# q and k projections of the seven-product blocks, computed token-major and transposed on TensorE

## The chip, the cores and the metric

The kernel runs on one core of a Trainium2 chip. The metric is the device time of one execution in microseconds (us). Three runs of the kernel before took 979.81, 979.97 and 980.25 us, with a median of 979.97.

## What is computed

One encoder layer on 512 tokens of width 2048, in f32. One input projection of 8192 columns gives q, k, v and a gate for each of two groups of 16 heads (head size 64):

```python
h = jnp.einsum('bsd,de->bse', x, w_in[layer])
qa, ka, va, ga, qb, kb, vb, gb = jnp.split(h, splits, axis=-1)
ya = _dilated_attention(heads(qa, N_HEADS_A), heads(ka, N_HEADS_A), heads(va, N_HEADS_A), t5_bias)
yb = _neighbourhood_attention(heads(qb, N_HEADS_B), heads(kb, N_HEADS_B), heads(vb, N_HEADS_B), na_rpb[layer])
ya = merge(ya) * jax.nn.silu(ga.astype(jnp.float32))
yb = merge(yb) * jax.nn.silu(gb.astype(jnp.float32))
y = jnp.concatenate([ya, yb], axis=-1).astype(x.dtype)
out = jnp.einsum('bse,ed->bsd', y, w_out[layer])
x = _layer_norm(DEEPNORM_ALPHA * x + out, ln_gain[layer], ln_bias[layer])
```

Group A attends over strided windows, group B over a two-dimensional neighbourhood. This case concerns only the projections to q and k of both groups: four matrices of 2048 x 1024, each multiplied with the 512 tokens.

## The kernel before

**Precision.** Each f32 operand of a large product is split into a high part (a rounded copy, made on ACT) and a low part (the rest, made on DVE), and a product is three matmuls: high x high, high x low, low x high. The function `split` and the helpers `high` (L364) and `low` (L369) do this.

**Stages.** Up to 71.03 us x is loaded and split and the first six gate tiles are computed (`plain_block`). Then come six seven-product blocks up to 546.82 us, in the order k, q, v of group A and k, q, v of group B. Behind them stand the attention, filled up with the other gate tiles (L516) and the first part of the output projection (L710), and last the rest of the output projection and the norm.

**A seven-product block** (`strassen_block`) cuts the matrix, the tokens and the depth into halves and needs seven products of half size instead of eight. The sums of halves of x are made once (`combine`); the sums of weights are made on DVE (L360) as each product comes up. A product has 8 depth slices of 128, handled in four steps of two (`run`, u = 0 to 3), and fills two PSUM banks, `accs[0]` and `accs[1]`. A block so has 28 steps.

In a v block the stationary operand is a slice of x (128 tokens) and 512 weight columns move: 12 matmuls a step (L384 to L386), and a bank holds 128 tokens x 512 channels. In a k or q block the stationary operand is a slice of the weights (128 channels) and 256 tokens move: 24 matmuls a step (L391 to L393), and a bank holds two tiles of 128 channels x 256 tokens. For k the tokens move in another order, (r b c) instead of (b r c), through a stepped read of x.

**The results.** The seven products are summed into four quarters of the result, named r1, w, u3 and c22, each in one SBUF tile with two halves t (`pair`). `keep` copies the first product on ACT, `combine_` makes four subtractions a half on DVE behind the fourth product (L406), and `plus` adds the fifth, sixth and seventh (L440). `store_kq` then splits a half into high and low (ACT and DVE) and writes it to DRAM, channel-major, with four transfers on SP's queue. The attention reads q and k from there.

**The order of the work** on PE, DVE and ACT is written out by hand (`manual_schedule` around `run_blocks`). At step n the loop issues the addition of weights for step n+3, ACT's high part for step n+2, then what `at` has put down for this step (the list `behind`), DVE's low part for step n+2, and last the matmuls of step n. There are three pairs of high and low buffers (`halves`), so ACT's copy for step n+2 waits for the matmuls of step n-1. SP and POOL are ordered by the planner of the language. PSUM has four buffers in `pacc`, two in `pss` and two in `pst` (the name pt); of the products, only the fourth in time (number 6) lies in `pst`, until `combine_` has read it.

Of the kernel before, what the change touches and what calls it, by code (L numbers as in the profile page):

```python
# [25 lines left out]
HALF = 256  # L26
# [44 lines left out]
def hybrid_layer(tc, xT, xn, w_in, w_early, w_gate, w_out, t5x, brow, rpb, cmask, eye, gain, lbias, out):  # L71
    nc = tc.nc
    from contextlib import ExitStack
    with ExitStack() as ctx:
# [6 lines left out]
        pst = ctx.enter_context(tc.tile_pool(name="pst", bufs=2, space=bass.MemoryType.PSUM))  # L81
# [44 lines left out]
        ident = const.tile([128, 128], F32, name="ident")  # L126
# [118 lines left out]
                        to = q_d[g][4 * ch + 2 * b + n][i].rearrange("c (b h q) -> c h b q", b=4, h=2)[:, half]  # L245
                        nc.sync.dma_start(to, f(o[:, i, n].rearrange("p (b q) -> p b q", b=4)))

        def store(kind, g, ch, half, t, src):
            if kind == "v":
                store_v(g, ch, half, t, src)  # L250
            else:
                store_kq(kind, g, ch, half, t, src)

        def silu(o, acc):

# [83 lines left out]
        jobs, behind = [], {}  # L339

        def strassen_block(src, kind, g, hooks):

            base = len(jobs)

            def load(q, tags):
                def run():
                    for u in range(4):
                        raw = slot(tags[u], F32, "braw")
                        nc.sync.dma_start(raw, src[4 * q + u])
                        raws[q].append(raw)  # L350
                return run

            raws = {q: [] for q in range(4)}

            def product(i, pool, q, other=None):
                accs = []

                def add(u):
                    if other is not None:
                        nc.vector.tensor_tensor(raws[q][u], raws[q][u], raws[other][u], ALU.add)  # L360

                def high(u):
                    h = halves.next("wh", F32R)
                    nc.scalar.activation(h, raws[q][u], AF.Copy)  # L364
                    return h

                def low(u, h):
                    l = halves.next("wl", F32R)
                    nc.vector.tensor_tensor(l, raws[q][u], f(h), ALU.subtract)  # L369
                    return h, l  # L370

                def run(u, h, l):
                    if u == 0:
                        accs.extend(bank(pool, "acc") for _ in range(2))
                    for t in range(2):
                        for kk in range(2):
                            k = 2 * u + kk
                            ah, al = operand(i, k)
                            if kind == "k":
                                ah, al = (m.rearrange("p (b r c) -> p r b c", r=4, b=4) for m in (ah, al))  # L380
                            if kind == "v":
                                c = slice(512 * kk, 512 * kk + 512)
                                q = slice(128 * t, 128 * t + 128)
                                nc.tensor.matmul(accs[t], ah[:, q], h[:, c], start=k == 0, stop=False)  # L384
                                nc.tensor.matmul(accs[t], al[:, q], h[:, c], start=False, stop=False)  # L385
                                nc.tensor.matmul(accs[t], ah[:, q], l[:, c], start=False, stop=k == 7)  # L386
                                continue
                            for n in range(2):
                                c = slice(512 * kk + 256 * t + 128 * n, 512 * kk + 256 * t + 128 * n + 128)
                                o = accs[t][:, HALF * n:HALF * n + HALF]  # L390
                                nc.tensor.matmul(o, h[:, c], ah, start=k == 0 and n == 0, stop=False)  # L391
                                nc.tensor.matmul(o, h[:, c], al, start=False, stop=False)  # L392
                                nc.tensor.matmul(o, l[:, c], ah, start=False, stop=k == 7 and n == 1)  # L393
                    if u == 3:
                        next(hooks, lambda: None)()

                jobs.extend((lambda u=u: add(u), lambda u=u: high(u), lambda h, u=u: low(u, h),
                             lambda h, l, u=u: run(u, h, l)) for u in range(4))
                return accs

            def at(product_, u, fn):

                behind.setdefault(base + 4 * product_ + u, []).append(fn)

            def sub(o, x, y):
                nc.vector.tensor_tensor(o, x, y, ALU.subtract)  # L406
# [24 lines left out]
            def combine_(t):  # L431
                r1, w, u3, c22 = (pair(n)[t] for n in ("r1", "w", "u3", "c22"))
                sub(w, r1, p6[t])
                sub(u3, w, p7[t])
                sub(c22, p5[t], u3)
                sub(w, p5[t], w)

            def plus(name, p, t):
                o = pair(name)[t]
                nc.vector.tensor_tensor(o, p[t], o, ALU.add)  # L440

            for t in range(2):
                at(1, t, lambda t=t: keep(t))
                at(4, t, lambda t=t: combine_(t))
                for n, name, p in ((5, "w", p3), (6, "r1", p2), (7, "u3", p4)):
                    at(n, t, lambda t=t, name=name, p=p: plus(name, p, t))
            for t in range(2):
                for n, name, ch, half in ((4, "c22", 1, 1), (5, "w", 1, 0), (6, "r1", 0, 0), (7, "u3", 0, 1)):
                    at(n, t + 1, lambda t=t, name=name, ch=ch, half=half: store(kind, g, ch, half, t, pair(name)[t]))
            sets[0], sets[2] = sets[2], sets[0]  # L450

        def run_blocks():
            ready = []
            for n in range(-4, len(jobs) + 4):
# [576 lines left out]
```

## Time and profile before

| | |
|---|---|
| median of 3 runs | 979.97 us |
| span of the profiled execution, first to last instruction | 978.4 us |
| PE busy | 968.1 us (99%) |
| DVE busy | 756.8 us (77%) |
| ACT busy | 486.6 us (50%) |
| six seven-product blocks | 71.03 to 546.82 us |
| mean granted TensorE clock | 0.996 |

The profile gives the profiled execution by its span of 978.4 us; the median of the runs lies 1.6 us above it. Busy time of PE counts a matmul from its start to a modelled end, and matmuls overlap: what a matmul costs in a full stream is the distance from its start to the next one's. Rows of the timeline show the start, the length, the engine, the line, the operation, the names out<-in, the shape and the count of merged instructions. Rows of the windows show the stretch, its length, busy time and count by engine (PE, weight loads PEld, DVE, ACT, POOL), the clock, the share of the DMA engines and GB/s.

### The profile page before, as it was taken

Reading aid. Unit: us, or ns where it says so; the run is one execution under the profiler, and the core shown is the slowest. Engines: PE = TensorE matmul, PEld = TensorE weight load, DVE = VectorE, ACT = ScalarE, POOL = GpSimd, SP = SyncE. Lnnn points to the kernel's source line nnn. Section 1 sums busy time; section 2 is a strip of 40 time slices with the busy share of each in tenths; the row PEclk is TensorE's granted clock in tenths of the full one; section 3 lists DMA queues with packets and bytes.
Section 4 is the critical chain, followed back from the end, with each engine's and each line's share of the span. In section 5 each row is a group of like instructions: output and inputs, shape, how many; then the busy total and the mean of one; then the engine's idle time right before and its main releaser. Section 6 shows DMA issues by size and latency. Waiting matters only on the chain.

```text
span 978.4 us, 16019 instructions
## 1 busy us (share of the span) xinstructions
PE 968.1 (99%) x5851; PEld 855.0 (87%) x5851; DVE 756.8 (77%) x1152; ACT 486.6 (50%) x839; POOL 179.0 (18%) x327
## 2 busy tenths in 40 slices
PE   9999999999999999999999999999999999999996
PEld 6889999999888999999888888888888888888885
DVE  7947788788988977878889567676676767777877
ACT  7534344344444434434454366666666666762300
POOL 1000665664553400000000001010010000100021
PEclk9999999999999999999999999999999999999998
DMA  9731688599569638428634967777777788768322
GB/s 341 289 120 55 164 276 270 177 255 273 178 188 302 185 95 277 116 87 232 165 120 113 343 185 217 194 232 234 188 222 224 197 238 205 209 223 293 90 75 97
DMA packets 118014, 194.29 MB, mean 199 GB/s; under 512 B 48351, under 2 KB 67551, under 8 KB 117936
## 3 DMA queue, kind: packets, MB, share of 16 engines
q1 hardware_dynamic: 105104, 169.15, 56.6%
q0 software_dynamic: 12256, 23.47, 8.7%
q8 instruction: 46, 0.75, 0.3%
q10 hardware_dynamic: 576, 0.66, 0.2%
q14 instruction: 32, 0.26, 0.1%
HBM read 148.68 MB, written 44.50 MB: 197 GB/s over the span
## 4 chain that ended last, share of the span: by engine, by line
PE 96%; DVE 1%; ACT 1%; DMA 1%; issue 0%; SPq 0%; DVEq 0%; ACTq 0%
PE acc L710 15%; PE acc L516 11%; PE acc L391 11%; PE acc L393 11%; PE acc L392 11%; PE acc L384 5%; PE acc L386 5%; PE acc L385 5%; PE pv L662 4%; PE pt L640 4%; PE acc L270 2%; PE sc L621 2%; PE acc L272 2%; PE acc L271 2%; PE sc L620 2%; PE sc L710 1%
## 5 line engine op out<-in xcount | busy, mean ns | idle before, releaser
L364 ACT ACTIVATE wh<-braw 128x1024 fp32r<-128x1024 f32 x168 | 178.3, 1061 | 254.9 <-PE acc L392 130.9
L369 DVE TENSOR_TENSOR wl<-braw,wh 128x1024 fp32r<-128x1024 f32 x168 | 206.4, 1229 | 65.6 <-ACT wh L364 65.3
L391 PE MATMUL acc<-xk,wh 128*128 128x256 f32 x512 | 144.5, 282 | 0.0
L393 PE MATMUL acc<-xk,wl 128*128 128x256 f32 x512 | 144.4, 282 | 0.0
L392 PE MATMUL acc<-xk,wh 128*128 128x256 f32 x512 | 144.4, 282 | 0.0
L360 DVE TENSOR_TENSOR braw<-braw 128x1024 f32<-128x1024 f32 x96 | 118.8, 1237 | 0.0
L710 PE MATMUL acc<-wh,yk 128*128 128x512 f32 x320 | 108.4, 402 | 0.0
L392 PE MATMUL acc<-op,wh 128*128 128x256 f32 x384 | 108.4, 282 | 0.0
L391 PE MATMUL acc<-op,wh 128*128 128x256 f32 x384 | 108.3, 282 | 0.0
L393 PE MATMUL acc<-op,wl 128*128 128x256 f32 x384 | 108.3, 282 | 0.0
L646 DVE TENSOR_TENSOR tl<-pt,th 128x256 fp32r<-128x256 f32 (+1 forms) x128 | 71.1, 555 | 48.0 <-ACT th L645 46.8
L391 PEld LDWEIGHTS acc<-xk,wh 128*128 128x128 f32 x512 | 97.2, 190 | 0.9 <-ACT bias L150 0.9
L392 PEld LDWEIGHTS acc<-xk,wh 128*128 128x128 f32 x512 | 97.2, 190 | 0.1
L393 PEld LDWEIGHTS acc<-xk,wl 128*128 128x128 f32 x512 | 97.2, 190 | 0.0
L645 ACT ACTIVATE th<-pt 128x256 fp32r<-128x256 f32 (+1 forms) x128 | 62.3, 489 | 65.0 <-PE pt L640 62.9
L516 PE MATMUL acc<-xk,wh 128*128 128x512 f32 x320 | 90.8, 402 | 0.0
L577 DVE CUSTOM_DVE_ANT_0 s<-sc,biases 128x512 f32<-128x512 f32 (+2 forms) x128 | 68.1, 532 | 17.9 <-PE sc L621 17.3
L581 ACT ACTIVATE p<-s,mn 128x512 f32<-128x512 f32 (+1 forms) x96 | 62.1, 647 | 25.6 <-DVE mn L577 25.2
L392 PEld LDWEIGHTS acc<-op,wh 128*128 128x128 f32 x384 | 72.9, 190 | 0.0
L393 PEld LDWEIGHTS acc<-op,wl 128*128 128x128 f32 x384 | 72.9, 190 | 0.0
L391 PEld LDWEIGHTS acc<-op,wh 128*128 128x128 f32 x384 | 72.9, 190 | 0.0
L710 PEld LDWEIGHTS acc<-wh,yk 128*128 128x128 f32 x320 | 58.4, 189 | 9.1 <-ACT yk L694 0.3
(183 smaller groups left out, 2026.1 us busy)
## 6 DMA issues: line engine op xcount, KB each, us to landing
braw<-in_w_in SPq DMA_DIRECT2D x96, 512.0 KB
wraw<-in_w_out SPq DMA_DIRECT2D x32, 512.0 KB
wraw<-in_w_gate SPq DMA_DIRECT2D x20, 512.0 KB
k_d<-kst SPq DMA_DIRECT2D x64, 128.0 KB
q_d<-kst SPq DMA_DIRECT2D x64, 128.0 KB
v_d<-vst SPq DMA_DIRECT2D x32, 256.0 KB
q<-q_d SPq DMA_DIRECT2D x32, 256.0 KB
k<-k_d SPq DMA_DIRECT2D x16, 512.0 KB
```

The source lines that it names most:

```text
L360: nc.vector.tensor_tensor(raws[q][u], raws[q][u], raws[other][u], ALU.add)
L364: nc.scalar.activation(h, raws[q][u], AF.Copy)
L369: nc.vector.tensor_tensor(l, raws[q][u], f(h), ALU.subtract)
L391: nc.tensor.matmul(o, h[:, c], ah, start=k == 0 and n == 0, stop=False)
L392: nc.tensor.matmul(o, h[:, c], al, start=False, stop=False)
L393: nc.tensor.matmul(o, l[:, c], ah, start=False, stop=k == 7 and n == 1)
L516: nc.tensor.matmul(acc, w[:, k * 128:k * 128 + 128], X[8 * u + k][:, s], start=u == 0 and n == 0 and k == 0, stop=u == 1 and n == 2 and k ...
L577: nc.vector.tensor_tensor_reduce(*flat, bias, 1.0, 3e38, ALU.add, ALU.min, mn)
L581: nc.scalar.activation(p[:, to:to + n].rearrange("p (b r c) -> p b r c", r=8, c=c), s[:, :n].rearrange(order, r=8, c=c), AF.Exp, bias=mn, ...
L645: nc.scalar.activation(th, pt[:, :nch], AF.Copy)
L646: nc.vector.tensor_tensor(tl, pt[:, :nch], f(th), ALU.subtract)
L710: nc.tensor.matmul(acc[:, part], yk[k][:, s, c], w[:, wk], start=first and kk == 0 and n == 0, stop=last and kk == 1 and n == 2)
```

## The change

All six blocks now compute token-major, as v did: x is stationary, 512 weight columns move, 12 matmuls a step. The seven products are summed as before, now with 128 tokens on the partitions and 512 channels in a row. For q and k each finished quarter is turned to channel-major by PE: for each of two groups b of 256 channels, four transposes of 128x128 write one PSUM bank `pt` (`turned_out`). For k they write the tokens in the order (r b c), in runs of 16 elements. `store_kq` reads that bank instead of the SBUF tile. The transposes of group b stand three steps behind the first addition to the quarter's half b, the store four steps; for v the store stays one step behind.

```diff
+        def turned_out(kind, two, b):
+            pt = bank(pst, "pt")
+            for n in range(2):
+                o = pt[:, HALF * n:HALF * n + HALF]
+                c = slice(256 * b + 128 * n, 256 * b + 128 * n + 128)
+                for t in range(2):
+                    if kind == "k":
+                        to = o.rearrange("p (r b c) -> p b r c", r=4, b=4)[:, 2 * t:2 * t + 2]
+                    else:
+                        to = o[:, 128 * t:128 * t + 128]
+                    nc.tensor.transpose(to, two[t][:, c], ident)
+            return pt
...
-                            if kind == "k":
-                                ah, al = (m.rearrange("p (b r c) -> p r b c", r=4, b=4) for m in (ah, al))
-                            if kind == "v":
-                                c = slice(512 * kk, 512 * kk + 512)
-                                q = slice(128 * t, 128 * t + 128)
-                                nc.tensor.matmul(accs[t], ah[:, q], h[:, c], start=k == 0, stop=False)
-                                nc.tensor.matmul(accs[t], al[:, q], h[:, c], start=False, stop=False)
-                                nc.tensor.matmul(accs[t], ah[:, q], l[:, c], start=False, stop=k == 7)
-                                continue
-                            for n in range(2):
-                                c = slice(512 * kk + 256 * t + 128 * n, 512 * kk + 256 * t + 128 * n + 128)
-                                o = accs[t][:, HALF * n:HALF * n + HALF]
-                                nc.tensor.matmul(o, h[:, c], ah, start=k == 0 and n == 0, stop=False)
-                                nc.tensor.matmul(o, h[:, c], al, start=False, stop=False)
-                                nc.tensor.matmul(o, l[:, c], ah, start=False, stop=k == 7 and n == 1)
+                            c = slice(512 * kk, 512 * kk + 512)
+                            q = slice(128 * t, 128 * t + 128)
+                            nc.tensor.matmul(accs[t], ah[:, q], h[:, c], start=k == 0, stop=False)
+                            nc.tensor.matmul(accs[t], al[:, q], h[:, c], start=False, stop=False)
+                            nc.tensor.matmul(accs[t], ah[:, q], l[:, c], start=False, stop=k == 7)
...
+            outs = {}
+            def turn_out(name, b):
+                outs[name, b] = turned_out(kind, pair(name), b)
             for t in range(2):
                 for n, name, ch, half in ((4, "c22", 1, 1), (5, "w", 1, 0), (6, "r1", 0, 0), (7, "u3", 0, 1)):
-                    at(n, t + 1, lambda t=t, name=name, ch=ch, half=half: store(kind, g, ch, half, t, pair(name)[t]))
+                    if kind == "v":
+                        at(n, t + 1, lambda t=t, name=name, ch=ch, half=half: store_v(g, ch, half, t, pair(name)[t]))
+                        continue
+                    at(n, t + 3, lambda t=t, name=name: turn_out(name, t))
+                    at(n, t + 4, lambda t=t, name=name, ch=ch, half=half: store_kq(kind, g, ch, half, t, outs.pop((name, t))))
...
-            for n in range(-4, len(jobs) + 4):
+            for n in range(-4, len(jobs) + 8):
```

How the order of instructions changes is shown at three places of the first k block. The first is PE's queue where the fifth product ends and the sixth begins. Before:

```order
L391 MATMUL acc<-op,wh 128x256
L392 MATMUL acc<-op,wh 128x256
L393 MATMUL acc<-op,wl 128x256
L391 MATMUL acc<-xk_106,wh 128x256
L392 MATMUL acc<-xk_106,wh 128x256
```

Of the change, with xk_106 the slice of x that the sixth product begins with and c_1153 the quarter c22:

```order
L389 MATMUL acc<-wh,op 128x512
L390 MATMUL acc<-wh,op 128x512
L391 MATMUL acc<-wl,op 128x512
L259 MATMUL pt<-ident,c_1153 128x2x4x16 x4
L389 MATMUL acc<-wh,xk_106 128x512
L390 MATMUL acc<-wh,xk_106 128x512
```

A group of four transposes now stands between the matmuls of two steps; its sisters for the other channel group stand 12 matmuls earlier, and the next two groups (w) 36 and 48 matmuls later.

The second place is DVE's queue from the last subtractions of `combine_` on. Before:

```order
L406 TENSOR_TENSOR c_1345<-acc,u_1344 128x512
L406 TENSOR_TENSOR w<-acc,w 128x512
L88 TENSOR_TENSOR kst<-c_1345,kst 128x512
L369 TENSOR_TENSOR wl<-braw,wh 128x1024
L88 TENSOR_TENSOR kst<-c_1345,kst 128x512
L369 TENSOR_TENSOR wl<-braw,wh 128x1024 x2
L440 TENSOR_TENSOR w<-acc,w 128x512
L369 TENSOR_TENSOR wl<-braw,wh 128x1024
```

Of the change:

```order
L404 TENSOR_TENSOR c_1153<-acc,u_1152 128x512
L404 TENSOR_TENSOR w<-acc,w 128x512
L377 TENSOR_TENSOR wl<-braw,wh 128x1024 x3
L438 TENSOR_TENSOR w<-acc,w 128x512
L88 TENSOR_TENSOR kst<-pt,kst 128x512
L377 TENSOR_TENSOR wl<-braw,wh 128x1024
```

The split of the stored quarter (kst) has left the place between the subtractions and the weights' split (wl) and stands three steps later, behind an addition.

The third place is SP's queue, where the first k block stores and the next block's weights are loaded. Before:

```order
L349 DMA braw<-in_w_in 128x1024 x7
L243 DMA k_d<-kst 64x2x256 x8
L349 DMA braw<-in_w_in 128x1024 x2
L243 DMA k_d<-kst 64x2x256 x4
L349 DMA braw<-in_w_in 128x1024
```

Of the change:

```order
L357 DMA braw<-in_w_in 128x1024 x8
L243 DMA k_d<-kst 64x2x256 x4
L357 DMA braw<-in_w_in 128x1024
L243 DMA k_d<-kst 64x2x256 x4
L357 DMA braw<-in_w_in 128x1024 x5
```

The stores have moved behind weight loads that they stood ahead of. The rest of SP's queue keeps its order but for such shifts between stores and loads; POOL's queue is the same.

More of the change, by code (lines that the diff above doesn't have):

```diff
@@ L246, in store_kq @@
                         nc.sync.dma_start(to, f(o[:, i, n].rearrange("p (b q) -> p b q", b=4)))
-        def store(kind, g, ch, half, t, src):
-            if kind == "v":
-                store_v(g, ch, half, t, src)
-            else:
-                store_kq(kind, g, ch, half, t, src)
+        def turned_out(kind, two, b):
[10 more added lines that the diff above has]
+            return pt
         def silu(o, acc):
@@ L378, in run @@
                             ah, al = operand(i, k)
-                            if kind == "k":
-                                ah, al = (m.rearrange("p (b r c) -> p r b c", r=4, b=4) for m in (ah, al))
-                            if kind == "v":
-                                c = slice(512 * kk, 512 * kk + 512)
-                                q = slice(128 * t, 128 * t + 128)
-                                nc.tensor.matmul(accs[t], ah[:, q], h[:, c], start=k == 0, stop=False)
-                                nc.tensor.matmul(accs[t], al[:, q], h[:, c], start=False, stop=False)
-                                nc.tensor.matmul(accs[t], ah[:, q], l[:, c], start=False, stop=k == 7)
-                                continue
-                            for n in range(2):
-                                c = slice(512 * kk + 256 * t + 128 * n, 512 * kk + 256 * t + 128 * n + 128)
-                                o = accs[t][:, HALF * n:HALF * n + HALF]
-                                nc.tensor.matmul(o, h[:, c], ah, start=k == 0 and n == 0, stop=False)
-                                nc.tensor.matmul(o, h[:, c], al, start=False, stop=False)
-                                nc.tensor.matmul(o, l[:, c], ah, start=False, stop=k == 7 and n == 1)
+                            c = slice(512 * kk, 512 * kk + 512)
[3 more added lines that the diff above has]
+                            nc.tensor.matmul(accs[t], ah[:, q], l[:, c], start=False, stop=k == 7)
                     if u == 3:
```

## The prediction

> **What bounds the kernel now.** First the page: busy shares, then the chain of waits by engine.
>
> ```profile
> PE 968.1 (99%) x5851; PEld 855.0 (87%) x5851; DVE 756.8 (77%) x1152; ACT 486.6 (50%) x839; POOL 179.0 (18%) x327
> ...
> PE 96%; DVE 1%; ACT 1%; DMA 1%; issue 0%; SPq 0%; DVEq 0%; ACTq 0%
> ```
>
> PE is the chain: whatever PE is spared is time, whatever it is given is time, and work on other engines counts only once PE waits for it. So I cut the stage that changes into its six blocks, with the table of windows: from the first product matmul of a block to that of the next, in the order k, q, v, k, q, v.
>
> ```profile
> core 0: us, PE busy (x) PEld busy (x) DVE busy (x) ACT busy (x) POOL busy (x), PEclk, DMA share, GB/s
> 71.03:152.55 81.52, 81.52 (x678) 79.85 (x676) 65.51 (x67) 35.93 (x41) 33.50 (x69) 1.00 0.61 179
> 152.55:233.18 80.63, 80.63 (x675) 80.63 (x673) 65.40 (x67) 34.83 (x38) 48.83 (x98) 1.00 0.80 239
> 233.18:309.37 76.19, 76.19 (x339) 63.07 (x337) 66.57 (x67) 34.88 (x38) 38.90 (x63) 1.00 0.75 221
> 309.37:390.00 80.63, 80.63 (x673) 80.63 (x672) 66.70 (x67) 34.80 (x38) 12.84 (x23) 1.00 0.61 189
> 390.00:470.63 80.63, 80.63 (x674) 80.63 (x673) 65.33 (x67) 34.83 (x38) 0.00 (x0) 1.00 0.54 158
> 470.63:546.82 76.19, 76.19 (x338) 63.07 (x337) 67.59 (x75) 37.77 (x46) 1.90 (x2) 1.00 0.49 146
> ```
>
> Every block keeps PE busy throughout at full clock. A k or q block is 672 matmuls of 256 moving columns: 80.63/672 = 0.1200 us each. A v block is 336 of 512: 76.19/336 = 0.2268. The same multiplications thus cost 4.44 us less in v's form; solved for both widths, a matmul costs 0.0132 us beside 0.417 ns a column, and 336 of these fixed parts go.
>
> The first k block is odd: the bias matmuls of L149 stand inside it.
>
> ```profile
> 93.95 0.28 PE L393 MATMUL acc<-op,wl 128*128 128x256 f32 x1
> 94.16 1.89 PE L149 MATMUL sc<-bias 33*16 33x512 f32 x4
> 95.98 0.39 PE L391 MATMUL acc<-xk,wh 128*128 128x256 f32 x1
> 96.20 0.28 PE L392 MATMUL acc<-xk,wh 128*128 128x256 f32 x1
> ```
>
> From 93.95 to 96.20 are 2.25 us for two matmuls that take 0.24, so the insertion costs 2.01. Without it the block takes 79.51 us, 1.12 under its sisters: a small bonus that the new form has no row for, so I let it go.
>
> **The change part by part.** *Removed and added matmuls.* Four blocks take v's form. Before they hold 81.52 + 3 x 80.63 = 323.41 us; in the new form 4 x 76.19 + 2.01 = 306.77. Saved: 16.64 us. The v windows measure exactly this, so I give it +-0.5 (the bonus of 1.12 and the insertion are its soft parts).
>
> A page speaks against this term. The Trainium skill, "TensorE: Matmul & The Clock Gate", section "Back-to-back issue gap", gives a warm gap of N/2.4 ns plus about 2.5 ns. By that the 1344 matmuls fewer would save an estimated 3.4 us, not 16.64; the two windows show 13.2 ns, and the measurement decides.
>
> *Added transposes.* Four sums a block, two channel groups each, four transposes a group: 32 groups, 128 transposes, all on PE. The nearest row is L640, the same operation on the same types and sizes (f32, 128x128, identity moving), also in groups of four between 512-wide matmuls.
>
> ```profile
> 565.43 0.60 PE L640 MATMUL pt<-ident,p 128*128 128x128 f32 x4
> 565.78 1.18 PE L516 MATMUL acc<-xk,wh 128*128 128x512 f32 x4
> 566.80 0.39 PE L620 MATMUL sc<-k,q 128*128 128x512 f32 x1
> 567.03 0.39 PE L621 MATMUL sc<-k,ql 128*128 128x512 f32 x1
> 567.26 1.32 PE L516 MATMUL acc<-xk,wh 128*128 128x512 f32 x5
> 568.42 0.60 PE L640 MATMUL pt<-ident,p 128*128 128x128 f32 x4
> ...
> 571.38 0.60 PE L640 MATMUL pt<-ident,p 128*128 128x128 f32 x4
> ```
>
> The group itself ends early (the next matmul starts 0.35 us after the first transpose), but the stream behind it runs slower than 0.2268 for a while. So I take the whole period less its matmuls, of which each of these two holds 11: 568.42 - 565.43 = 2.99, less 11 x 0.2268 = 2.495, leaves 0.495; 571.38 - 568.42 = 2.96, less the same, leaves 0.465. Mean 0.48 a group. In the change two groups are 12 matmuls apart, then 36, so each has room for the whole slow stretch: I take 0.48, and 32 x 0.48 = 15.4 us. Below, a group cannot cost nothing (its rows hold PE); where the next group cuts the slow stretch off, the least is seen:
>
> ```profile
> 854.22 0.60 PE L640 MATMUL pt<-ident,p 128*128 128x128 f32 x4
> ...
> 855.80 0.49 PE L640 MATMUL pt<-ident,p 128*128 128x128 f32 x3
> ```
>
> With five matmuls between, 855.80 - 854.22 - 5 x 0.2268 = 0.45, or 14.4 us in all. Above, each transpose could hold PE for its whole recorded length:
>
> ```profile
> L640 PE MATMUL pt<-ident,p 128*128 128x128 f32 x320 | 50.5, 272 | 0.0
> L646 DVE TENSOR_TENSOR tl<-pt,th 128x512 fp32r<-128x512 f32 x64 | 44.2, 691 | 27.6 <-ACT th L645 26.7
> L88 DVE TENSOR_TENSOR kst<-r,kst 128x512 fp32r<-128x512 f32 x4 | 2.8, 692 | 4.0 <-ACT kst L87 4.0
> L645 ACT ACTIVATE th<-pt 128x512 fp32r<-128x512 f32 x64 | 38.1, 597 | 34.9 <-PE pt L640 33.4
> L87 ACT ACTIVATE kst<-r 128x512 fp32r<-128x512 f32 x4 | 2.5, 614 | 0.0
> ```
>
> 128 x 0.272 = 34.8 us; the spacing above excludes it.
>
> *The stores' split* now reads PSUM. DVE's L646 does that in 691 ns against 692 from SBUF, ACT's L645 in 597 against 614: nothing.
>
> *Later stores.* In program order the transposes of a sum stand three steps behind its first addition, the store four, where it was one. (A step is a quarter of a product: 12 matmuls, 2.72 us.) Is PE held by them? The second half of a sum is made two steps ahead of the transposes, and on DVE it stands before the split of the weights that this same step needs anyway: no new wait. Are ACT and DVE held? In a v block ACT mostly waits for PE already, because a weight buffer comes free only when the previous step's matmuls are done:
>
> ```profile
> ACT wh L364 <- PE acc L385: 31.0, 20, 1.7
> ```
>
> The transposes stand ahead of those matmuls, so they are done when ACT gets to the store. Nothing queued behind it (ACT's next weight copy, DVE's next split) waits longer. DVE's tightest place is the four subtractions after the fourth product, here in the first v block:
>
> ```profile
> 282.04 0.68 DVE L406 TENSOR_TENSOR w<-acc,w 128x512 f32<-128x512 f32 x1
> 282.63 0.69 DVE L223 TENSOR_TENSOR vst<-c,vst 128x512 fp32r<-128x512 f32 x1
> 283.23 1.22 DVE L369 TENSOR_TENSOR wl<-braw,wh 128x1024 fp32r<-128x1024 f32 x1
> ```
>
> These weights end at 284.45; PE needs them in the third matmul of its step 19, at 233.18 + 19 x 2.72 + 0.45 = 285.3. So 0.9 us of cover, with a store in between that the new k and q blocks have moved away: 0.60 more. DVE's 66.57 of 76.19 us held PE up nowhere, and the changed blocks give it about 65.4 of 80.
>
> *SP and the loads.* The stores keep their 128 transfers and now stand behind weight loads that they stood ahead of, so no load is later for it, and POOL's order is unchanged: nothing. PSUM's two pt buffers hold the fourth product in time until step 17 and are next asked for at 19: no wait.
>
> **The sum.** 16.64 - 15.4 = 1.2 us less. The profiled span of 978.4 becomes 977.2; the median of the runs is 979.97, 1.6 above the span, which I leave as it is: 978.7 us. Its own range, with 0.45 to 0.50 a group and +-0.5 on the saving, is 977.2 to 979.8.
>
> **The rivals.**
>
> *Cheaper groups.* If a stream of one kind recovers as fast as the cut-off rows suggest (0.45), the cost is 14.4, the gain 2.2 and the time 977.7. For it: the changed stream has no other shapes between. Against it: the full periods show 0.465 and 0.495. Chance 0.22.
>
> *Stepped writes cost, slower.* k's transposes write their outputs in runs of 16 elements, q's in one run. Half the transposes, 64, are concerned. If a stepped output doubles their pace of about 0.109 us (four of them within 0.60 from first start to last end, each 0.272 long), that adds 64 x 0.109 = 7.0 us: 985.7, slower. It eats the gain from 0.019 us a transpose on. Nearest rows: of each four L662 here, one writes two runs of 128.
>
> ```profile
> 594.23 0.64 PE L662 MATMUL pv<-th,vv 128*128 128x256 f32 x4
> 594.70 0.64 PE L662 MATMUL pv<-tl,vv 128*128 128x256 f32 x4
> 595.18 0.40 PE L516 MATMUL acc<-xk,wh 128*128 128x512 f32 x1
> ```
>
> Four take 0.47 or 0.48 us, 0.119 each as for plain 256-wide ones, so long runs cost nothing; runs of 16 have no row. Chance 0.09.
> The Trainium skill, "PSUM — Partial Sum Buffer", section "Specifications (TRN2)", holds that any non-contiguous access pattern slows matmuls significantly; these L662 rows don't show it.
>
> *DVE becomes the bound, slower.* The store's split waits on a transpose and holds the weights' split behind it. It decides once that hold passes the 1.5 us of cover; half a microsecond beyond it in each of 16 pairs is 8 us, 986.7. Against it: the order above and two v blocks without a gap. Chance 0.08.
>
> *The width saves nothing, slower.* Were the windows' difference due to something particular to v and not to the width, nothing would be saved and the time would be 979.97 + 15.4 = 995.4. The gate and output matmuls have w as weights and x moving at 512 and run at 0.2268 too (16 of L516 from 546.82 to 550.45):
>
> ```profile
> 546.82 3.79 PE L516 MATMUL acc<-xk,wh 128*128 128x512 f32 x16
> 550.45 1.98 PE L516 MATMUL acc<-xk,wl 128*128 128x512 f32 x8
> ```
>
> Chance 0.03. The Trainium skill's gap rule, named above, leads to this side: by its estimated 3.4 us of saving the time would be 992.
>
> **How the numbers follow.** The forecast has 0.58. 0.2% of 979.97 is 1.96 us, about what a measurement of this kernel tells from no change, so faster means under 978.0. Faster: the cheaper groups, 0.22. Slower: 0.07 of the stepped writes, 0.05 of the bound DVE and the 0.03 of the last rival, 0.15. The rest, 0.58 with 0.02 and 0.03 of mild forms, is within 0.2%: 0.63. The range goes from 977.2, where the cheaper groups come with the saving's upper end, to 981.6, where the stepped writes cost 0.045 us each; it leaves out the strong forms of the slower rivals and little below.
>
> **What would show it.** Three of a block's eight groups fall into the block behind it. So the table of windows should give about 76.2 + 5 x 0.48 = 78.6 us for a k block (the first one 2.0 more), 76.2 + 8 x 0.48 = 80.0 for a q block, 76.2 + 3 x 0.48 = 77.6 for a v block, with PE busy throughout. A period of transposes in the stream should be 0.48 over its matmuls, the same in k and q; k above q would show the stepped writes. PE idle with DVE's wl as the releaser would show the third rival; matmuls at other than 0.2268 the fourth. I am wrong if the slow stretch behind a group is longer or shorter in this stream than in the attention stage, or if a wait appears on PE.

## The result, and the profile after

The changed kernel takes **978.25 us** (median of 21 runs, 977.85 to 978.93), the kernel before beside it 979.89 (21 runs, 979.39 to 980.25): a ratio of **0.9984**, 95% interval 0.9978 to 0.999. That is 1.6 us or 0.16% less, within the 0.2% that the prediction counted as no change, and 0.45 us under its 978.7.

The page of the changed kernel, busy shares and the chain of waits by engine:

```profile
PE 967.1 (99%) x4635; PEld 799.2 (82%) x4635; DVE 756.1 (77%) x1152; ACT 486.0 (50%) x839; POOL 178.6 (18%) x327
...
PE 96%; DVE 1%; ACT 1%; DMA 1%; issue 0%; SPq 0%; DVEq 0%; ACTq 0%
```

PE has 1216 instructions fewer (1344 matmuls out, 128 transposes in) and is as busy as it was. The windows of the six blocks, k, q, v, k, q, v, with columns as before:

```profile
70.97:151.96 80.99, 80.99 (x365) 65.55 (x364) 64.33 (x65) 35.10 (x40) 34.14 (x70) 1.00 0.60 176
151.96:231.99 80.03, 80.03 (x372) 66.22 (x370) 64.99 (x66) 34.58 (x39) 49.59 (x99) 1.00 0.79 240
231.99:309.25 77.26, 77.26 (x348) 63.95 (x345) 68.48 (x68) 35.42 (x40) 41.99 (x67) 1.00 0.78 219
309.25:388.17 78.92, 78.92 (x361) 65.34 (x360) 65.21 (x66) 34.12 (x37) 7.90 (x17) 1.00 0.59 192
388.17:468.20 80.03, 80.03 (x372) 66.21 (x370) 64.99 (x66) 34.58 (x39) 0.00 (x0) 1.00 0.55 159
468.20:545.46 77.26, 77.26 (x347) 63.95 (x346) 68.31 (x76) 38.32 (x48) 1.91 (x2) 1.00 0.51 148
```

PE is busy throughout, at full clock. The six blocks sum to 474.49 us against 475.79 before (546.82 - 71.03): **1.30 us less, where the sum gave 1.28** (16.64 - 15.36). The rest of the program gives the other 0.3 of the span's 978.4 - 976.8. Outside the blocks two profiles of one kernel differ by more (0.7 us in the two of the kernel with eight transposes in a group, below), so no cause is claimed for it.

What a group of transposes costs is read from the timeline of PE: two sums of a k block, the last group of that block, and two sums of the q block behind it.

```profile
360.93 0.60 PE L259 MATMUL pt<-ident,c 128*128 128x128 f32 x4
...
372.78 0.60 PE L259 MATMUL pt<-ident,w 128*128 128x128 f32 x4
...
387.59 0.39 PE L391 MATMUL acc<-wl,xk 128*128 128x512 f32 x1
387.82 0.60 PE L259 MATMUL pt<-ident,r 128*128 128x128 f32 x4
388.17 0.48 PE L389 MATMUL acc<-wh,xk 128*128 128x512 f32 x1
...
440.96 0.60 PE L259 MATMUL pt<-ident,c 128*128 128x128 f32 x4
441.31 0.48 PE L389 MATMUL acc<-wh,op 128*128 128x512 f32 x1
441.63 0.39 PE L390 MATMUL acc<-wh,op 128*128 128x512 f32 x1
...
452.80 0.60 PE L259 MATMUL pt<-ident,w 128*128 128x128 f32 x4
```

From one sum's first group to the next sum's there are two groups and 48 matmuls, 48 x 0.2268 = 10.89. In q, 452.80 - 440.96 = 11.84 leaves 0.95, or **0.48 a group**, as forecast; in k, 372.78 - 360.93 = 11.85 leaves 0.48 again, so the runs of 16 elements cost nothing. The group at 387.82 stands ahead of q's first matmul and so still belongs to k's window. The groups of a k, q and v window are therefore 6, 8 and 2, not the forecast's 5, 8 and 3: 76.19 + 6 x 0.48 = 79.07 (78.92 measured), 80.03 (80.03), 77.15 (77.26). The total is the same.

The stores' operations and the waits of PE, where the first two rows are groups by tile (least, median and greatest length in ns, first and last start) and the other two PE's only waits over 1 us (us in all, times, longest), both outside the blocks:

```profile
L87 ACT ACTIVATE kst<-pt x16: 573/578/582, 128.8 to 403.9; 128x512 fp32r<-128x512 f32 x16
L88 DVE TENSOR_TENSOR kst<-pt,kst x16: 678/692/693, 129.5 to 404.5; 128x512 fp32r<-128x512 f32 x16
```

```profile
PE pt L916 <- DVE nms L914: 2.5, 1, 2.5
PE sc L124 <- POOL calm L121: 1.3, 1, 1.3
```

The stores' splits from PSUM take no longer than they took from SBUF (692 ns on DVE both ways; 578 against 614 on ACT), and the list of PE's waits has no entry of the six blocks.

### The profile page after: what moved, and what is told of

Read it like the earlier page. It is cut to its first block, busy times and chain, and to the rows that moved or that the text cites. A ratio compares the mean times of both kernels' runs of the same rounds, so it can differ in the third digit from the quotient of the medians.

```text
span 976.8 us, 13613 instructions
## 1 busy us (share of the span) xinstructions
PE 967.1 (99%) x4635; PEld 799.2 (82%) x4635; DVE 756.1 (77%) x1152; ACT 486.0 (50%) x839; POOL 178.6 (18%) x327
## 4 chain that ended last, share of the span: by engine, by line
PE 96%; DVE 1%; ACT 1%; DMA 1%; issue 0%; SPq 0%; DVEq 0%; ACTq 0%
PE acc L389 16%; PE acc L391 16%; PE acc L390 16%; PE acc L717 15%; PE acc L523 11%; PE pv L669 4%; PE pt L647 4%; PE acc L278 2%; PE sc L628 2%; PE acc L279 2%; PE acc L280 2%; PE sc L627 2%; PE pt L259 1%; PE sc L717 1%; PE pt L717 1%; DMA xraw<-in_xT 1%
## 5 line engine op out<-in xcount | busy, mean ns | idle before, releaser
L389 PE MATMUL acc<-wh,xk 128*128 128x512 f32 x384 | 151.9, 396 | 0.0
L391 PE MATMUL acc<-wl,xk 128*128 128x512 f32 x384 | 149.8, 390 | 0.0
L390 PE MATMUL acc<-wh,xk 128*128 128x512 f32 x384 | 149.6, 390 | 0.0
L389 PE MATMUL acc<-wh,op 128*128 128x512 f32 x288 | 112.8, 392 | 0.0
L391 PE MATMUL acc<-wl,op 128*128 128x512 f32 x288 | 112.2, 390 | 0.0
L390 PE MATMUL acc<-wh,op 128*128 128x512 f32 x288 | 112.1, 389 | 0.0
L391 PEld LDWEIGHTS acc<-wl,xk 128*128 128x128 f32 x384 | 72.1, 188 | 15.4
L389 PEld LDWEIGHTS acc<-wh,xk 128*128 128x128 f32 x384 | 72.1, 188 | 15.1 <-ACT bias L150 0.9
L390 PEld LDWEIGHTS acc<-wh,xk 128*128 128x128 f32 x384 | 72.2, 188 | 14.3
L523 PEld LDWEIGHTS acc<-xk,wh 128*128 128x128 f32 x320 | 57.0, 189 | 9.5
L160 POOL DMA_DIRECT2D bias<-rows_d x128 | 61.5, 488 | 16.2 <-DMA bias<-rows_d 6.4
L717 PE MATMUL acc<-wl,yk 128*128 128x512 f32 x160 | 63.9, 403 | 0.0
```

Of the source, the lines that this page charges most:

```text
L523: nc.tensor.matmul(acc, w[:, k * 128:k * 128 + 128], X[8 * u + k][:, s], start=u == 0 and n == 0 and k == 0, stop=u == 1 and n == 2 and k ...
L717: nc.tensor.matmul(acc[:, part], yk[k][:, s, c], w[:, wk], start=first and kk == 0 and n == 0, stop=last and kk == 1 and n == 2)
```

## The experiments

The two terms of the sum were each 12 to 13 times as large as their difference, so the first runs measure each alone.

### The transposes left out

```diff
-                    at(n, t + 3, lambda t=t, name=name: turn_out(name, t))
-                    at(n, t + 4, lambda ...: store_kq(kind, g, ch, half, t, outs.pop((name, t))))
+                    at(n, t + 4, lambda ...: store_kq(kind, g, ch, half, t, pair(name)[t]))
```

> The changed kernel without its 128 transposes: the stores read the token-major sums, so q and k reach the attention with tokens and channels exchanged (that part of the computation is left out); all else stands where it stood. Theory (PE alone sets the time, a group of four costs 0.475 to 0.485 us): 32 x 0.48 = 15.4 us less than the changed kernel's 978.25, 962.9 us, and all six blocks at 76.2 us between their first matmuls (the first one 2.0 more). Rival (part of the transposes' cost is a hand-over between PE and DVE, or is hidden): a saving clearly other than 15.4 and idle PE or DVE at other places; if each transpose held PE for its whole recorded 0.272 us, 34.8 us less, 943.5.

Measured: 964.69 us (2 runs, 962.7 to 966.69), ratio 0.9848 [0.9829, 0.9867]. The windows of its first two blocks:

```profile
70.82:149.02 78.20, 78.20 (x342) 63.28 (x340) 63.98 (x65) 34.92 (x39) 33.51 (x69) 1.00 0.59 171
149.02:225.18 76.16, 76.16 (x338) 63.06 (x336) 64.66 (x67) 34.86 (x38) 45.74 (x93) 1.00 0.82 246
```

All blocks but the first take 76.16, the first 2.04 more for the bias matmuls; the six sum to 78.20 + 5 x 76.16 = 459.00. So the form alone saves 475.79 - 459.00 = 16.79 us (16.64 forecast), and the transposes give back 474.49 - 459.00 = **15.49** (15.36 forecast). Both terms stand. The median lies only 13.6 under the changed kernel's, but the two runs are 4 us apart; the windows are those of the run of 962.7, where 962.9 was forecast.

### The same operands in halves of 256 columns

For q and k x stays stationary and the transposes stay, but each matmul moves 256 weight columns in place of 512. It parts the width from what else is particular to v's form.

```diff
-                            nc.tensor.matmul(accs[t], ah[:, q], h[:, c], ...)
...
+                            for n in range(1 if kind == "v" else 2):
+                                w = 512 if kind == "v" else 256
+                                o = accs[t][:, w * n:w * n + w]
+                                c = slice(512 * kk + w * n, 512 * kk + w * n + w)
+                                nc.tensor.matmul(o, ah[:, q], h[:, c], ...)
...
```

> The changed kernel with one thing undone: in the q and k blocks each 512-column matmul is issued as two of 256 columns, x still the stationary operand. Theory (each matmul has a fixed 0.0132 us beside its columns, whatever it holds): four blocks x 336 x 0.0132 = 17.8 us more, 996.0 us; k block of group B from 78.93 to 83.4, q block from 80.03 to 84.5. Rival (v's form is quick because x is the stationary operand): no change, 978.25.

Measured: 994.72 us (2 runs), ratio 1.0154 [1.0136, 1.0173]. Its first two windows:

```profile
70.64:155.80 85.16, 85.16 (x702) 83.50 (x700) 64.55 (x65) 34.96 (x40) 34.20 (x71) 1.00 0.61 176
155.80:239.91 84.11, 84.11 (x708) 84.11 (x706) 65.14 (x66) 34.55 (x39) 53.00 (x105) 1.00 0.79 225
```

The timeline of the second q block has the starts of these matmuls 0.120 us apart:

```profile
440.47 0.28 PE L393 MATMUL acc<-wh,op 128*128 128x256 f32 x1
440.59 0.28 PE L394 MATMUL acc<-wh,op 128*128 128x256 f32 x1
```

At that pace 672 of them are the 80.63 us of a q block before, which leaves (84.11 - 80.63)/8 = 0.435 for each of the eight groups. With x stationary the pace is thus the same 0.1200 as with the weights stationary: what saves is the width, that is, half as many matmuls, each with 13.2 ns beside its columns (0.1200 against 0.2268 us). Every matmul here brings its own weight load, so twice as many matmuls are also twice as many loads, and no run parts these two. The measured windows sum to 490.97, 16.5 above the changed kernel's, where 17.8 was forecast: a group costs 0.435 among these narrower matmuls and not 0.48.

The Trainium skill's rule of 2.5 ns ("TensorE: Matmul & The Clock Gate", section "Back-to-back issue gap"), named in the prediction as speaking against this term, would have put this run an estimated 3.4 us above the changed kernel. The Trainium skill gives the rule there for an isolated matmul, and the prediction took it for a stream; in this stream the measured 16.5 us decide.

### Every group made twice

```diff
-            for n in range(2):
+            for n in (0, 1, 0, 1):
```

> The changed kernel with each group of four transposes done twice, the second time over the first's results in the same bank. Theory (a further transpose costs its spacing of 0.1085 us; the slow stretch behind a group is paid once): 128 x 0.1085 = 13.9 us more, 992.1; k block of group B 78.93 + 5 x 0.434 = 81.1, q block 80.03 + 8 x 0.434 = 83.5, k's and q's transposes at one price. Rival (a group of four costs 0.48 each time): 15.4 more, 993.6. Rival (stepped writes of k are dearer and hid beside something): k's group of eight above q's.

Measured: 992.66 us (2 runs), ratio 1.0131 [1.0112, 1.0149]. Windows of its second k and q block:

```profile
316.46:397.99 81.53, 81.53 (x386) 68.00 (x384) 64.51 (x65) 34.44 (x37) 5.58 (x13) 1.00 0.55 179
397.99:481.43 83.44, 83.44 (x404) 69.74 (x401) 65.39 (x66) 34.56 (x39) 0.00 (x0) 1.00 0.54 152
```

Against the changed kernel k takes 81.53 - 78.92 = 2.61 more for 24 further transposes, q 3.41 for 32: 0.109 and 0.107 each. In all, the windows sum to 488.08, 13.59 more for 128 transposes, 0.106 each. The group's price of 0.48 is thus four times 0.107 and 0.05 for the slower stream behind it, and a transpose that writes runs of 16 elements costs what a plain one does: the rival of the stepped writes has no ground left. The Trainium skill ("PSUM — Partial Sum Buffer", section "Specifications (TRN2)") has any non-contiguous access pattern in PSUM slow a matmul significantly; k against q here does not show it.

### Eight transposes in one group

If 0.05 of a group is the slow stretch behind it, both channel groups turned together should pay that once.

```diff
-                    at(n, t + 3, lambda t=t, name=name: turn_out(name, t))
+                    at(n, 3, lambda t=t, name=name: turn_out(name, t))
```

> The changed kernel with the eight transposes of a quarter in one group, three steps behind its first addition, instead of two groups of four a step apart; the stores stay where they are. Theory (a group has a fixed part: 0.48 less four spacings of 0.1085 = 0.046 us): 16 groups fewer, 16 x 0.046 = 0.7 us less, 977.5; the q block of group B from 80.03 to 79.7. Rival (a transpose costs 0.12 us wherever it stands): no change, 978.25. Second rival (the second bank is not free so early): PE idle before the second four, 979 or more.

Measured: 978.18 us (11 runs, 977.3 to 980.72), ratio 0.9988 [0.998, 0.9997]. Its second k and q windows, then two waits of the attention stage in the profiled execution:

```profile
308.93:387.84 78.91, 78.91 (x362) 65.55 (x360) 65.53 (x65) 33.67 (x36) 17.01 (x23) 1.00 0.60 184
387.84:467.64 79.80, 79.80 (x370) 66.38 (x368) 65.11 (x66) 34.57 (x38) 0.00 (x0) 1.00 0.56 163
```

```profile
DVE y L700 <- DMA rc<-rc_d: 1.6, 1, 1.6
```

```profile
PE pt L678 <- DVE den L806: 1.0, 1, 1.0
```

The blocks sum to 473.52, 0.97 less than the changed kernel's, which is 16 stretches at 0.06. But the median of the runs was only 0.07 below the changed kernel's. In the profiled execution, which took 979.26, DVE waited for a transfer and PE for DVE at about 764 us, in the attention. I took that wait to vary from run to run and so ran this kernel and the changed one once more, side by side.

> The same kernel as e3_group8, timed again beside the changed kernel on one chip. Its blocks ended 0.77 us earlier than the changed kernel's, its median only 0.07. Theory (chance: the attention stage waits some 1 us on a transfer of the softmax shares in some runs): median 0.5 to 0.8 us below the changed kernel's. Rival (the earlier start meets that transfer every time): no difference.

> The changed kernel itself, timed in the same rounds as e12_group8_again. Theory: 978.2 us, blocks ending at 545.5 us in the profile.

Measured: 978.01 us (11 runs, 977.55 to 979.14) with eight, 978.79 (12 runs, 977.68 to 984.97) for the changed kernel; ratios to before 0.9982 [0.9973, 0.9991] and 0.9986 [0.9977, 0.9995]. The medians lie 0.78 apart, in the direction and about the size of the windows' 0.96, yet the intervals overlap: the windows show the gain, the total does not settle it. Nor is the wait in the attention all that hides it: the profile with eight transposes has no such wait, and its span is still 976.8, the changed kernel's own in the first profile; its blocks began 0.4 us later (71.35 against 70.97), and what follows them took 0.6 more (431.9 against 431.3). The profiled execution of the changed kernel was its slowest run, and tells what the wait in the attention can do. DVE's and PE's waits there, and windows of 4 us around it:

```profile
DVE y L700 <- DMA rc<-rc_d: 4.9, 1, 4.9
```

```profile
PE pt L678 <- DVE den L806: 4.2, 1, 4.2
```

```profile
760.00:764.00 4.00, 3.89 (x19) 2.80 (x18) 0.70 (x4) 1.30 (x4) 0.00 (x0) 1.00 0.86 243
764.00:768.00 4.00, 0.00 (x0) 0.00 (x0) 2.43 (x7) 1.10 (x3) 0.00 (x0) 0.89 1.05 212
768.00:772.00 4.00, 3.94 (x17) 3.60 (x17) 2.37 (x7) 3.71 (x9) 0.52 (x1) 0.50 0.83 190
772.00:776.00 4.00, 4.00 (x18) 3.26 (x17) 3.54 (x6) 1.73 (x3) 1.05 (x2) 0.75 0.08 23
```

DVE waited 4.9 us for the transfer, PE stood for 4.2, and then ran at half clock: the last two rows have means of 0.50 and 0.75, and a window of 767.13 to 773.96 has 0.50, the next one 1.00 again. What follows the blocks took 438.1 us in place of 431.3, so beside the 4.2 of the wait some 2.5 went that way: the span is 983.2. Its six blocks sum to 474.48, as in the other profile of this kernel. So a total of this kernel can differ by microseconds for a reason that lies behind the change, and comparisons under 1 us are made by windows.

### Transposes and stores two steps earlier

The prediction costed the wait on DVE at nothing because the transposes stand three steps behind the addition they read. This run takes two of the three away.

```diff
-                    at(n, t + 3, lambda t=t, name=name: turn_out(name, t))
-                    at(n, t + 4, lambda ...: store_kq(...))
+                    at(n, t + 1, lambda t=t, name=name: turn_out(name, t))
+                    at(n, t + 2, lambda ...: store_kq(...))
```

> The changed kernel with the transposes and stores two steps earlier: the first group of a quarter one step behind its first addition. Theory (the three steps are what hides DVE): PE now waits for the second half of each quarter, about 2.6 us for c22 and 1.3 for each of w, r1 and u3, 6.5 us a block, 26 us in all if none of it is made up: 985 to 1004, with idle PE ahead of each quarter's first group and DVE's sums as the releaser. Rival (the sums are ready anyway and the distance is free): 978.25.

Measured: 1013.46 us (2 runs, 1010.38 to 1016.54), ratio 1.0343 [1.0312, 1.0374]: the waits are the expected ones, the total is above the expected 985 to 1004. PE's waits, and its timeline at the first sum of the second k block:

```profile
PE pt L259 <- DVE c L404: 9.8, 4, 2.5
PE pt L259 <- DVE r L438: 4.9, 4, 1.2
PE pt L259 <- DVE u L438: 4.7, 4, 1.2
PE pt L259 <- DVE w L438: 4.7, 4, 1.2
```

```profile
372.08 0.27 PE L259 MATMUL pt<-ident,c 128*128 128x128 f32 x1
374.81 0.90 PE L259 MATMUL pt<-ident,c 128*128 128x128 f32 x3 [2.46 <-DVE c L404]
375.36 0.78 PE L389 MATMUL acc<-wh,op 128*128 128x512 f32 x1
...
376.79 0.63 PE L389 MATMUL acc<-wh,op 128*128 128x512 f32 x1
377.21 0.63 PE L390 MATMUL acc<-wh,op 128*128 128x512 f32 x1
```

The 16 waits sum to 24.1 us. They are the wait that the prediction asked about under the later stores ("Is PE held by them?"): the transposes need DVE's second half of the sum, and at one step's distance it isn't there yet. It is the distance that hides it, not spare time on DVE. The blocks grew by 508.48 - 474.49 = 34 us, so some 10 beyond the waits. The list counts a wait from the end of the transpose before it; from start to start the 16 cost 26.8 (2.72 or about 1.47 each, less the 0.109 of a transpose in the stream). The other 7 are pace: behind each wait of 2.5 us the matmuls start 0.42 us apart in place of 0.2268 for about 3 us; behind waits of 1.2 they do not. A window behind the wait that ends at 374.81 shows the clock:

```profile
374.81:378.22 3.41, 3.41 (x10) 2.83 (x11) 1.67 (x2) 0.00 (x0) 0.00 (x0) 0.50 0.36 115
```

The granted clock is 0.50 there, for 3.41 us; in the stretch of the same length behind it is 1.00 again.

### Why the first k block gained nothing

The prediction let go a bonus: without the bias matmuls the first k block ran 1.12 us quicker than its sisters, and I had no reason for it. It matters, for against 79.51 + 2.01 the first block gains only 3.3 us and not 4.4, less than the 3.84 of its eight groups. The theory: an instruction of another kind shifts PE's stream, and the stepped read of x that k has keeps the shift to the end of the block. Its test puts one f32 transpose of the identity ahead of the second k and q blocks of the kernel before.

```diff
+            if g == 1 and kind != "v":
+                at(0, 0, lambda: nc.tensor.transpose(bank(pst, "pt")[:, 0:128], ident, ident))
```

> The kernel before, with one f32 transpose of the identity put ahead of the first matmul of the k block and of the q block of group B. Question: why the first k block ran at 0.1177 us a matmul behind the bias matmuls and the others at 0.1200. Theory (an f32 instruction shifts PE's stream, and the stepped read of k keeps the shift): the k block of group B falls from 80.63 to about 79.3 us, the q block, with a plain read, stays at 80.6 to 80.9; in all about 1 us less, 978.9. Rival (the quick pace belongs to the first block's place or its neighbours): both blocks at 80.6 to 80.9, 980.3 in all.

Measured: 978.35 us (10 runs, 978.04 to 979.29), ratio 0.9986 [0.9977, 0.9996]. Windows of the second k and q blocks:

```profile
309.34:388.50 79.16, 79.16 (x676) 79.16 (x674) 66.77 (x67) 34.83 (x38) 13.41 (x22) 1.00 0.61 190
388.50:469.21 80.71, 80.71 (x675) 80.71 (x674) 65.37 (x67) 34.82 (x38) 0.00 (x0) 1.00 0.54 160
```

One instruction more, and the k block takes 1.47 us less (80.63 before): 672 matmuls at 0.1178 in place of 0.1200. That is a mean: in the timeline the distances of the slow pace are 0.120 throughout, those of the quick one lie between 0.111 and 0.121. The q block, with the same instruction ahead of it, stays at 0.1200. One line gives about what the whole change gave.

k's matmuls differ from q's in the stepped read of x; and the instruction ahead might have to be f32. The next run takes these apart in the kernel before: ahead of the second k block a short matmul of the same rounded type as the stream, and in the second q block, behind an f32 transpose, the plain read with a stepped write to PSUM.

```diff
+                                if kind == "q" and g == 1:
+                                    o = o.rearrange("p (b r c) -> p r b c", r=4, b=4)
...
+            if g == 1 and kind == "k":
+                at(0, 0, lambda: nc.tensor.matmul(bank(pst, "pt")[:, 0:128], X[0][:, 0, 0:128], X[0][:, 0, 0:128], ...))
+            if g == 1 and kind == "q":
+                at(0, 0, lambda: nc.tensor.transpose(bank(pst, "pt")[:, 0:128], ident, ident))
```

> The kernel before with two probes in group B. Ahead of the k block (stepped read) one short f32r matmul of 128 columns in place of the f32 transpose; ahead of the q block an f32 transpose, with q's read left plain and only its PSUM write stepped (q of group B so holds its tokens in another order: its values are left out of the computation's result). Theory (an f32 instruction shifts, a stepped read keeps the shift): k block at 80.6 to 80.8 us, q block at 80.7. Rival (any short instruction shifts): k block at 79.2. Rival (the stepped write keeps the shift): q block at 79.2.

Measured: 978.66 us in one run. The same two windows:

```profile
309.56:388.66 79.10, 79.10 (x675) 79.10 (x674) 66.70 (x67) 34.81 (x38) 12.47 (x22) 1.00 0.62 192
388.66:469.38 80.72, 80.72 (x675) 80.72 (x674) 65.37 (x67) 34.82 (x38) 0.00 (x0) 1.00 0.55 159
```

The short matmul does it as well as the f32 transpose, so the theory that it takes f32 is out, and a stepped write does not keep it. So what these runs need is one instruction more ahead, of either of the two kinds tried, and a stepped read. That the instruction shifts the stream is a picture; by which mechanism a stepped read keeps the quick pace, these runs do not show.

### The first k block in the old form

Since the first k block already ran quickly, the change was left out there alone.

```diff
+            old = kind == "k" and g == 0
...
+                            if old:
+                                ah, al = (m.rearrange("p (b r c) -> p r b c", r=4, b=4) for m in (ah, al))
...
+                    if old:
+                        at(n, t + 1, lambda ...: store_kq(kind, g, ch, half, t, pair(name)[t]))
```

> The changed kernel with the first k block left as it was before (256 tokens moving, no transposes). Theory (that block had the quick pace of 0.1177 us and so gains 3.3 us by the width less 8 x 0.48 = 3.8 for its groups): the first k block back at 81.5, the q block behind it without three spilled groups at 78.6, together 160.1 against 161.0: 0.9 us less than the changed kernel, 977.4. Rival (all four blocks gain alike, 0.4 us each): 978.6 or more.

Measured: 977.81 us (11 runs, 977.29 to 978.38), ratio 0.9979 [0.997, 0.9988]. Its first two windows:

```profile
71.12:152.64 81.52, 81.52 (x678) 79.85 (x676) 65.52 (x67) 35.92 (x41) 33.49 (x69) 1.00 0.62 177
152.64:231.63 78.99, 78.99 (x363) 65.39 (x361) 64.23 (x65) 34.01 (x37) 50.01 (x100) 1.00 0.79 241
```

The k block gives back 0.53 and the q block behind it is spared 1.04: two groups of k's, not the three that the expectation put there by the prediction's 5, 8, 3. The blocks sum to 473.98, 0.51 under the changed kernel. So in the first k block the change loses: eight groups (3.84) for 3.3 saved.

### A version that beats both

If the shift is worth 1.5 us in a k block, a q block can have it too: the kernel before, channel-major, with one transpose ahead of every k and q block but the first, q's tokens read in k's stepped order and written back to PSUM in their own.

```diff
-                            if kind == "k":
+                            if kind != "v":
                                 ah, al = (m.rearrange("p (b r c) -> p r b c", r=4, b=4) for m in (ah, al))
...
+                                if kind == "q":
+                                    o = o.rearrange("p (b r c) -> p r b c", r=4, b=4)
...
+            if kind != "v" and base:
+                at(0, 0, lambda: nc.tensor.transpose(bank(pst, "pt")[:, 0:128], ident, ident))
```

> The kernel before, channel-major and without the change, with an f32 transpose of the identity ahead of the second, third and fourth of its k and q blocks, and with q's tokens read in k's stepped order and written to PSUM in a stepped order that undoes it. Theory (the shift lasts while the moving read is stepped): these three blocks at 79.2 us each in place of 80.63, 4.4 us less than before, 975.5. Rival (the shift belongs to k, not to the read): q blocks at 80.7, 978.4 as with the single kicked k block. Rival (q's stepped write disturbs): q blocks above 80.7.

Measured: **975.22 us** (5 runs, 974.81 to 975.73), ratio **0.9952** [0.9938, 0.9965]. Its first q block and its second k and q blocks:

```profile
152.67:231.79 79.12, 79.12 (x675) 79.12 (x674) 65.20 (x67) 34.85 (x38) 48.21 (x97) 1.00 0.80 242
...
308.01:387.16 79.15, 79.15 (x675) 79.15 (x674) 66.75 (x67) 34.84 (x38) 12.03 (x23) 1.00 0.63 191
387.16:466.29 79.13, 79.13 (x676) 79.13 (x674) 65.22 (x67) 34.86 (x38) 0.00 (x0) 1.00 0.56 164
```

Three blocks at 79.13 against 80.63: the six sum to 471.35, 4.4 us under before and 3.1 under the changed kernel, with 3 transposes in place of its 128 and without the later stores.

## Why the prediction was right

- *The bound*: right. PE was the chain before and is after, and every microsecond of the blocks' sum is PE's stream.
- *Saved by the form, 16.64*: 16.79 by the run without transposes. By the run with halves it comes of the width and not of what is stationary; whether the weight loads or the matmuls themselves make up the 13.2 ns is open. Within it the first k block saves 3.3 and the others 4.47 each; the forecast had that in the sum, but called the quick pace of the first block a bonus without a row. The runs gave it its two conditions, an odd instruction ahead and a stepped read, and left the mechanism open.
- *Given back by the transposes, 15.4*: 15.49. That the difference of the two terms came out within 0.02 us is partly luck: each was short, by 0.15 and 0.13, and the two errors cancel. The price of 0.48, read from whole periods in the attention stage, holds in this stream for k and q alike. *Cheaper groups* (0.45) did not come: a group pays its slow stretch each time unless the next group follows at once.
- *Stores' split, later stores, SP, loads: nothing*: right, with no wait of PE in the blocks. The run with earlier transposes shows what the cover was: at one step's distance 24.1 us of waiting on the list, and 34 in all with what the list leaves out and the half clock.
- *Stepped writes*: not so, 0.48 in both, and 0.109 against 0.107 when doubled. *DVE becomes the bound*: not so; what came at one step's distance was PE waiting for an addition, not the weights' split. *The width saves nothing*: not so.
- *Where it was off*: the windows of k and v. "Three of a block's eight groups fall into the block behind it" should have been two, as one stands just ahead of the next block's first matmul: 78.92 and 77.26 for the forecast's 78.6 and 77.6, nothing in the total. And 0.45 us of the total lies outside the blocks or in the runs' spread.

## What to carry to other kernels

When a change trades one cost on the bound engine for another of the same size, price both from whole periods of the stream, from one event to the next, and not from recorded lengths (a transpose is recorded at 272 ns and costs 107). A wait hidden by distance is not a slack of the engine waited for, so the distance is part of the change. And a block that runs a per cent quicker than its sisters for no known reason is worth one run before anything else: here it held about three times what the change gave.

## What the hardware showed that was not expected

- One instruction more (an f32 transpose or a short matmul) ahead of a run of 256-column matmuls with a stepped read takes them from 0.1200 to 0.1178 us on average for the 672 that follow. With a plain read it does nothing (80.71 and 80.72 against 80.63), and a stepped write doesn't replace the stepped read.
- PE's pace after idling: 1.2 us idle, twelve times, cost nothing more. 2.5 us idle, four times, each brought 3.41 us at a granted clock of 0.50, and 4.2 us idle brought twice that, 6.83. The Trainium skill ("TensorE: Matmul & The Clock Gate", section "Part 1: The HAM clock gate (the "warmup" mystery)") has the clock halved after an idle window of about 3.4 us. The length of the slow stretches agrees, but PE need not idle for the whole of it: in the 3.41 us ahead of 374.81 it was busy for 0.95.
- A transpose group leaves the stream of 512-column matmuls behind it slower by 0.05 us in all, once per group, whether it has four transposes or eight (0.48 and about 0.90). Among 256-column matmuls that stretch did not show: 0.435 a group, four times 0.109.
